# One layer pair on one core: bias rows and inverse blocks passed through DRAM in packed form

## Chip, cores and metric

The kernel runs on one core of one Trainium2 chip. The metric is device time in microseconds, the median of several runs. Times inside an execution are microseconds from the start of its span.

## What is computed

The input is a sequence of 512 tokens of width 1024. A first block (retention, short convolution, three-way sparse attention, gated merge, gated feed-forward with a convolution) and a second block (gated delta rule, sliding-window attention, gated merge, gated feed-forward) are applied in turn. Two pieces of the second block matter here.

The delta rule solves a unit lower triangular system for each chunk of 64 tokens, 4 heads by 8 chunks:

```python
a_mat = jnp.where(strict_lower, jnp.einsum("bhncd,bhnsd->bhncs", k_beta, kc) * decay, 0.0)
lhs = a_mat + jnp.eye(C, dtype=a_mat.dtype)
sol = lax.linalg.triangular_solve(lhs, rhs, left_side=True, lower=True, unit_diagonal=True)
```

The sliding-window branch adds a learned bias that depends only on the distance of query and key, with 8 heads, blocks of 128 queries and 256 keys for each:

```python
dist = SWA_BLOCK + qi - kj
in_window = (dist >= 0) & (dist < WINDOW_2)
bias = rel_bias.astype(jnp.float32)[t5_causal_bucket(dist)]
logits = jnp.where(mask[None, :, None, None], logits + bias, -jnp.inf)
```

## The kernel before, in words

Activations are kept as 128 features by 512 tokens. Each fp32 matrix product runs as three products of rounded high and low parts: `weight` (L274) loads a tile of 128x1024 on SP's queue (L285, two buffers), ScalarE makes the high part `wh` (L268), VectorE the low part `wl` (L269, three buffers each), and `gemm` (L290) issues 24 products of 128x512 (L262) into one of two accumulators `g`. VectorE empties an accumulator in `scaled` (L389). The order on each engine's queue is fixed when the program is built: the framework's scheduler takes the instructions in program order, but moves later ones forward where it reckons them ready. `after` (L234) only tells that scheduler to keep an instruction behind another. An engine takes its queue in order.

**The bias rows.** While the first feed-forward (`ffn1`, L836, 22 turns n, two `gemm` each) runs, `bias_rows(n)` (L1181) is called at the end of each turn. For n = 0 it loads the 32 bucket values of the 8 heads and a one-hot matrix. For n = 1 a product gives 8 rows of 384 bias values, and VectorE copies them to SBUF (L1196). For n = 2 a transfer on GpSimd's queue writes each row 128 times to the DRAM tile `bd` of [8, 128, 384]. For n = 10 to 17 eight transfers write zeros to the DRAM tile `dn_x`. In each turn the gated product is formed on GpSimd (L849), and ScalarE and VectorE split it (L271, L272) into `gh` and `gl`, which only the next stage reads. `bias_table` (L1203) later reads `bd` with a row step of 383, so that partition p has the rows shifted by p: the table `tab` of 128 queries, 8 heads, 256 keys. `swa_head` (L1251) adds it to the scores on VectorE (L1274 for 256 keys, L1276 for the first block's 128).

**The inverse blocks.** `dn_inverse` (L1060) forms 16 strictly lower matrices of 128x128 and writes them to the DRAM tile `dn_n`. `dn_blocks` (L1042) reads the 128 diagonal blocks of 16x16 back, one to a partition (tile N), and inverts them by 15 steps of two VectorE operations (L1053, L1054) into Y. It then writes Y onto the diagonal blocks of the zeroed `dn_x` (L1055) and reads the whole, 16 matrices of 128x128, back as X (L1057), all on SP's queue. `dn_inverse` transposes X on TensorE (L1094) and doubles the inverted blocks to 32, 64 and 128 by products and corrections (L1105, L1109). Between these small products the scheduler sets products of later functions, of `dn_values`, `nat2` and `gates2`, as filler on TensorE.

Of the kernel before, what the change touches and what calls it, by code (L numbers as in the profile page):

```python
# [68 lines left out]
def constants():  # L69
    p = np.arange(128)  # L70
    c = {}
    c["ident"] = np.eye(128)
    c["causal"] = np.concatenate([np.zeros((128, 384)), np.where(p[None] <= p[:, None], 0.0, BIG)], 1)
    t = np.arange(512).reshape(4, 128).T
    cc = np.arange(32)
    c["cmask"] = np.where((16 * cc + 31 <= t[:, :, None]) & (cc < 31), 0.0, -BIG).reshape(128, 128)
    c["any1"] = (p >= 31)[:, None] * np.ones((1, 1))
    theta = 10000.0 ** (-np.linspace(0.0, 1.0, 64, dtype=np.float32))
    ang = np.arange(512, dtype=np.float32)[None, :] * theta.astype(np.float32)[:, None]
    co, si = np.cos(ang.astype(np.float64)), np.sin(ang.astype(np.float64))  # L80
    c["rotc"] = np.concatenate([co, co], 0)
    c["rots"] = np.concatenate([si, -si], 0)
    lg = np.log1p(-(2.0 ** (-5.0 - np.arange(RH))))
    rel = np.arange(512)[None, :] - p[:, None]
    dec = [np.where(rel >= 0, np.exp(lg[h] * np.maximum(rel, 0)), 0.0) * 128 ** -0.5 for h in range(RH)]
    c["decay"] = np.concatenate(dec, 1)
    c["triu"] = (p[:, None] <= p[None, :]) * 1.0
    c["mstrict"] = np.where(p[None, :] < p[:, None], 0.0, -BIG)
    c["mincl"] = np.where(p[None, :] >= p[:, None], 0.0, -BIG)
    lev = []  # L90
    for b in (16, 32, 64):
        cols = (np.arange(64 // b)[:, None] * 2 * b + np.arange(b)[None]).reshape(-1)
        same = (p[:, None] // (2 * b)) == (cols[None] // (2 * b))
        lev.append((same & (p[:, None] % (2 * b) >= b)) * 1.0)
    c["levels"] = np.concatenate(lev, 1)
    c["band"] = (p[:, None] // 32 == np.arange(4)[None]) * 1.0
    return {k: _f(v) for k, v in c.items()}


CONST = constants()  # L100
C_SETS = [["ident"], ["causal", "cmask", "any1", "band"], ["triu", "mstrict", "mincl", "levels"]]
C_OFF, C_LEN = {}, []
for _k, _s in enumerate(C_SETS):
    _o = 0
# [5 lines left out]

def onehot():
    r = np.arange(384)
    dist = 255 - r
    n = np.maximum(dist, 0)
    nf = np.maximum(n, 1).astype(np.float32)
    large = 16 + (np.log(nf / np.float32(16)).astype(np.float32) / np.float32(math.log(8.0)) * np.float32(16)).astype(np.int32)
    large = np.minimum(large, BUCKETS - 1)
    b = np.where(n < 16, n, large)
    m = np.zeros((BUCKETS + 1, 384), np.float32)
    ok = (dist >= 0) & (dist < 128)  # L120
    m[b[ok], r[ok]] = 1.0
    m[BUCKETS, ~ok] = 1.0
    return m
# [72 lines left out]
class Kern:  # L196
# [639 lines left out]
    def ffn1(self):  # L836
        nc, A = self.nc, self.A
        gh, gl = self.units(NF, F32R), self.units(NF, F32R)
        for n in range(NF):
            ta = self.scaled(self.gemm(A["w_fu"][n, 0], self.xh, self.xl))  # L840
            a = self.tmp()
            self.conv(a, ta, V_FC, 3, 44, n)
            th = ta
            nc.scalar.activation(th, a, AF.Tanh, scale=0.5)
            tv = self.scaled(self.gemm(A["w_fu"][n, 1], self.xh, self.xl))
            v = self.tmp()
            self.conv(v, tv, V_FC, 3, 44, NF + n)
            nc.vector.scalar_tensor_tensor(a, th, 1.0, a, op0=OP.add, op1=OP.mult)
            nc.gpsimd.tensor_mul(a, a, v)  # L849
            self.split(gh(n), gl(n), a, 0.5)  # L850
            self.bias_rows(n)
        return gh, gl

    def block1(self):
# [187 lines left out]
    def dn_blocks(self, dn):  # L1042
        nc = self.nc
        zz = lambda: self.sp.tile([128, 16, 16], F32, name="zz", bufs=3)
        N, Y, W = zz(), zz(), zz()
        blocks = lambda d: bass.AP(tensor=d.tensor, offset=d.offset, ap=[[PITCH // 8, 128], [128, 16], [1, 16]])
        nc.sync.dma_start(N, blocks(dn))
        self.after(nc.vector.memset(Y, 0.0), self.last)
        nc.vector.memset(Y.rearrange("p r c -> p (r c)")[:, 0:256:17], 1.0)
        for j in range(15):  # L1050
            a, b = 15 - j, j + 1
            w = W.rearrange("p r c -> p (r c)")[:, :a * b].rearrange("p (r c) -> p r c", c=b)
            nc.vector.tensor_mul(w, N[:, b:, j:b].to_broadcast([128, a, b]), Y[:, j:b, 0:b].to_broadcast([128, a, b]))  # L1053
            self.chain = nc.vector.tensor_sub(Y[:, b:, 0:b], Y[:, b:, 0:b], w)  # L1054
        nc.sync.dma_start(blocks(self.dn_x), Y)  # L1055
        X = self.unit(shape=(128, 16, 128))
        nc.sync.dma_start(X, self.rows_of(self.dn_x))  # L1057
        return X

    def dn_inverse(self):  # L1060
# [117 lines left out]
            nc.vector.tensor_mul(y[:, t], y[:, t], z[:, t])  # L1178
        return y.rearrange("p t h c -> p t (h c)")

    def bias_rows(self, n):  # L1181

        nc, A = self.nc, self.A
        if n == 0:
# [1 line left out]
            rb, oh = self.early[:BUCKETS + 1, 0:8], self.early[:BUCKETS + 1, 128:512]  # L1186
            self.load(rb, A["relb"], self.last)
            self.load(oh, A["oneh"], self.last)
            self.after(nc.gpsimd.memset(self.early[:, 1024:1152], 0.0), self.last)
            self.bias = self.dp.tile([8, 128, 384], F32, name="bd")  # L1190
            self.dn_x = self.dp.tile([16, PITCH], F32, name="dn_x")
        elif n == 1:
            rb, oh = self.early[:BUCKETS + 1, 0:8], self.early[:BUCKETS + 1, 128:512]
            p = self.ps("o", 1)
            self.mm(p[:8, :384], rb, oh, True, True)
            nc.vector.tensor_copy(self.early[:8, 512:896], p[:8, :384])  # L1196
        elif n == 2:
            self.load(self.bias, self.early[:8, None, 512:896].to_broadcast([8, 128, 384]), self.last)
        elif 10 <= n < 18:
            m = slice(2 * (n - 10), 2 * (n - 10) + 2)  # L1200
            self.load(self.rows_of(self.dn_x, m), self.early[:, None, 1024:1152].to_broadcast([128, 2, 128]), self.last)

    def bias_table(self):  # L1203
        self.tab = self.unit(shape=(128, 8, 256))
        dr = self.bias
        src = bass.AP(tensor=dr.tensor, offset=dr.offset + 127, ap=[[383, 128], [128 * 384, 8], [1, 256]])
        self.load(self.tab, src, self.last)

    def swa_proj(self):
# [41 lines left out]
    def swa_head(self, j, s):  # L1251
# [11 lines left out]
        for u in range(2):  # L1263
            lg = self.sp.tile([128, 512], F32, name="sm", bufs=2).rearrange("p (a c) -> p a c", a=2)
            for v in range(2):
# [5 lines left out]
                self.mm(S, st[:, qs], KS[:, 2 + s, k0:k0 + 256], False, True)  # L1271
                i = (j * 4 + nb) * 2 + s
                if nb:
                    nc.vector.scalar_tensor_tensor(lg[:, v, :], S, rr[:, i:i + 1], self.tab[:, h, :], op0=OP.mult, op1=OP.add)  # L1274
                else:
                    nc.vector.scalar_tensor_tensor(lg[:, 0, 128:256], S[:, 0:128], rr[:, i:i + 1], self.tab[:, h, 128:256],  # L1276
                                                   op0=OP.mult, op1=OP.add)
                    nc.gpsimd.tensor_scalar(lg[:, 0, 0:128], lg[:, 0, 128:256], 0.0, -BIG, op0=OP.mult, op1=OP.add)
            us = slice(2 * u, 2 * u + 2)
# [112 lines left out]
```

## Time and profile before

| what | us |
|---|---|
| median of 3 runs | 2077.3 (2075.71 to 2077.73) |
| the profiled execution, own time | 2075.4 |
| its span, first to last instruction | 2073.6 |
| TensorE busy | 2022.6 |
| VectorE busy | 1215.2 |
| ScalarE busy | 846.8 |
| GpSimd busy | 243.7 |

The profile is of one execution. PE is TensorE, PEld its weight loads, DVE is VectorE, ACT ScalarE, POOL GpSimd, SP the engine whose queue issues weight loads. In a row `out<-in` names the tiles, buffer numbers left out: `g`, `s`, `t`, `o` are accumulators, `wf` a loaded weight tile, `u` a large SBUF tile. A bracket at the end of a row gives the idle time of the engine before it and what ended it. "x2" is the number of instructions merged into a row.

### The profile page before, as it was taken

How to read it: one execution, taken by the hardware profiler on the slowest of the kernel's cores; microseconds unless marked ns; L12 is line 12 of the kernel's file. 1: busy time of each engine (PE TensorE's matmuls, PEld its weight loads, DVE VectorE, ACT ScalarE, POOL GpSimd, SP SyncE). 2: the span in 40 equal slices, each digit the busy share in tenths (PEclk: the TensorE clock that was granted, in tenths of full speed). 3: DMA queues.
4: the chain of work that ended last, by engine and by line, in shares of the span. 5: the costliest groups of instructions: out<-in, count | busy, mean ns of one | idle time of the engine just before them, and what ended most of it. 6: DMA issues, size and time to landing. Idle time of an engine off the chain costs nothing.

```text
span 2073.6 us, 26727 instructions
## 1 busy us (share of the span) xinstructions
PE 2022.6 (98%) x10184; PEld 1693.5 (82%) x10184; DVE 1215.2 (59%) x2238; ACT 846.8 (41%) x1530; POOL 243.7 (12%) x369
## 2 busy tenths in 40 slices
PE   7999999999999999998999999999999999999999
PEld 6878888888899888886788888878878878888887
DVE  7477877864525645565777634794557675444422
ACT  4466767742132323332444423553545342222221
POOL 3010011000301111111111100010000121111100
PEclk9999999999999999999999999999999999999999
DMA  6121111123232232344233343322221252322442
GB/s 240 45 72 51 52 52 52 42 83 101 92 108 78 80 99 85 117 157 103 86 108 105 110 136 119 101 77 76 72 82 36 80 184 97 102 93 100 123 126 76
DMA packets 63280, 196.91 MB, mean 95 GB/s; under 512 B 11373, under 2 KB 13549, under 8 KB 62640
## 3 DMA queue, kind: packets, MB, share of 16 engines
q1 hardware_dynamic: 54720, 167.24, 25.2%
q0 software_dynamic: 7712, 26.78, 4.5%
q8 instruction: 80, 1.31, 0.3%
q10 hardware_dynamic: 720, 1.19, 0.2%
q14 instruction: 48, 0.39, 0.1%
HBM read 182.98 MB, written 12.19 MB: 94 GB/s over the span
## 4 chain that ended last, share of the span: by engine, by line
PE 86%; DVE 7%; DMA 3%; ACT 2%; issue 1%; POOL 1%; ACTq 0%; POOLq 0%; DVEq 0%; SPq 0%
PE g L262 72%; PE s L262 5%; PE o L262 5%; DVE wl L269 2%; PE t L656 1%; ACT wh L268 1%; PE t L262 1%; DMA wf<-in_w_fu 1%; DVE w L424 1%; DMA u<-in_xT 1%; DVE u L272 0%; DMA u<-dn_x 0%; PE t L1289 0%; POOL w L591 0%; PE t L698 0%
## 5 line engine op out<-in xcount | busy, mean ns | idle before, releaser
L262 PE MATMUL g<-u,wh 128*128 128x512 f32 x4464 | 1404.9, 393 | 24.7 <-DVE w L389 13.7
L262 PEld LDWEIGHTS g<-u,wh 128*128 128x128 f32 x4464 | 835.6, 189 | 195.3 <-issue 14.4
L262 PE MATMUL g<-u,wl 128*128 128x512 f32 x2232 | 874.7, 392 | 0.2 <-DVE wl L269 0.2
L268 ACT ACTIVATE wh<-wf 128x1024 fp32r<-128x1024 f32 (+4 forms) x325 | 331.7, 1021 | 774.6 <-PE g L262 551.9
L269 DVE TENSOR_TENSOR wl<-wf,wh 128x1024 fp32r<-128x1024 f32 (+4 forms) x325 | 403.7, 1242 | 229.4 <-ACT wh L268 226.2
L262 PEld LDWEIGHTS g<-u,wl 128*128 128x128 f32 x2232 | 420.5, 188 | 85.5 <-DVE wl L269 1.2
L262 PE MATMUL g<-wh,u 128*128 128x256 f32 (+2 forms) x736 | 142.9, 292 | 0.0
L389 DVE TENSOR_TENSOR w<-g,R 128x512 f32<-128x512 f32 x104 | 71.5, 689 | 116.9 <-PE g L262 116.5
L262 PEld LDWEIGHTS g<-wh,u 128*128 128x128 f32 x736 | 117.1, 191 | 1.0 <-DVE u L744 0.2
L424 DVE SCALAR_TENSOR_TENSOR w<-w,vecs 128x510 f32<-128x510 f32 (+1 forms) x140 | 105.6, 754 | 2.9 <-ACT w L422 0.8
L262 PE MATMUL g<-wl,u 128*128 128x256 f32 (+2 forms) x368 | 106.7, 290 | 0.0
L262 PE MATMUL o<-u 128*128 128x256 f32 (+1 forms) x418 | 83.4, 297 | 2.3 <-issue 1.4
L262 PEld LDWEIGHTS o<-u 128*128 128x128 f32 x418 | 61.3, 188 | 14.8 <-ACT u L268 4.6
L262 PE MATMUL s<-u,st 128*128 128x256 f32 (+2 forms) x288 | 71.7, 335 | 0.1
L262 PEld LDWEIGHTS g<-wl,u 128*128 128x128 f32 x368 | 70.2, 191 | 0.8
L268 ACT ACTIVATE u<-t 128x512 fp32r<-128x512 f32 (+1 forms) x112 | 58.2, 528 | 11.0 <-PE t L698 6.3
L1322 POOL TENSOR_TENSOR w<-w,R 128x512 f32<-128x512 f32 x22 | 39.0, 1772 | 198.5 <-ACT w L1321 198.5
L271 ACT ACTIVATE u<-w 128x512 fp32r<-128x512 f32 x44 | 27.3, 623 | 68.2 <-POOL w L849 68.1
L849 POOL TENSOR_TENSOR w<-w 128x512 f32<-128x512 f32 x22 | 28.3, 1284 | 226.2 <-DVE w L424 211.3
L272 DVE SCALAR_TENSOR_TENSOR u<-w,u 128x512 fp32r<-128x512 f32 x44 | 30.2, 689 | 40.9 <-ACT u L271 40.9
L422 ACT ACTIVATE w<-w,vecs 128x512 f32<-128x512 f32 x64 | 46.2, 721 | 19.6 <-DVE w L389 15.0
L262 PEld LDWEIGHTS s<-u,st 128*128 128x128 f32 x288 | 47.0, 189 | 5.3 <-DVE sm L1276 0.5
(376 smaller groups left out, 1914.3 us busy)
## 6 DMA issues: line engine op xcount, KB each, us to landing
wf<-in_w_fu SPq DMA_DIRECT2D x44, 512.0 KB, 3.5
wf<-in_x_gu SPq DMA_DIRECT2D x44, 512.0 KB, 3.7
wf<-in_w_sc SPq DMA_DIRECT2D x24, 512.0 KB, 3.6
wf<-in_w_mg SPq DMA_DIRECT2D x24, 512.0 KB, 3.6
wf<-in_w_fd SPq DMA_DIRECT2D x16, 512.0 KB, 3.6
wf<-in_x_gt SPq DMA_DIRECT2D x16, 512.0 KB, 3.7
wf<-in_x_dn SPq DMA_DIRECT2D x16, 512.0 KB, 3.6
x<-st POOLq DMA_DIRECT2D x24, 256.0 KB, 2.4
```

The costliest lines, as they stand in the source:

```text
L262: self.last = self.nc.tensor.matmul(out, l, r, start=start, stop=stop)
L268: nc.scalar.activation(hi, src, AF.Copy)
L269: nc.vector.tensor_sub(lo, src, hi.bitcast(F32))
L271: nc.scalar.activation(hi, src, AF.Copy, scale=scale)
L272: return nc.vector.scalar_tensor_tensor(lo, src, scale, hi.bitcast(F32), op0=OP.mult, op1=OP.subtract)
L389: self.nc.vector.tensor_mul(t, p, self.R)
L422: nc.scalar.activation(dst, src, AF.Copy, scale=self.vec(w + (nt - 1) * stride + j))
L424: nc.vector.scalar_tensor_tensor(dst[:, i:], src[:, :T - i], self.vec(w + (nt - 1 - i) * stride + j), dst[:, i:], op0=OP.mult, op1=OP.add)
L656: nc.tensor.transpose(pt[:, c:c + 128], parts[v][:, k * 128:(k + 1) * 128], self.ident)
L849: nc.gpsimd.tensor_mul(a, a, v)
L1322: nc.gpsimd.tensor_mul(t, t, self.R)
```

## The change

The one-hot matrix is built for distances that rise along the row (r - 128 in place of 255 - r), and the 8 rows of 384 are written once to DRAM, in the call for n = 1. The table is read with a row step of one element, so that neighbouring partitions read overlapping pieces of the same rows, and `swa_head` reads the table backwards along the keys (step -1). The inverted blocks are written to DRAM as they lie (128 blocks of 256 numbers) and read back with 16 numbers for each row and matrix (tile XB, 128x16x16). Four multiplications on VectorE, one for each group of four matrices, spread XB over the 128 columns of X with a mask of 128x8 block indicators, which joins the constants. The zeroed `dn_x`, its zero fills and their memset go.

```diff
--- before.py
+++ after.py
@@ -94,11 +94,12 @@
         lev.append((same & (p[:, None] % (2 * b) >= b)) * 1.0)
     c["levels"] = np.concatenate(lev, 1)
     c["band"] = (p[:, None] // 32 == np.arange(4)[None]) * 1.0
+    c["diag"] = (p[:, None] // 16 == np.arange(8)[None]) * 1.0
     return {k: _f(v) for k, v in c.items()}
 
 
 CONST = constants()
-C_SETS = [["ident"], ["causal", "cmask", "any1", "band"], ["triu", "mstrict", "mincl", "levels"]]
+C_SETS = [["ident"], ["causal", "cmask", "any1", "band"], ["triu", "mstrict", "mincl", "levels", "diag"]]
 C_OFF, C_LEN = {}, []
 for _k, _s in enumerate(C_SETS):
     _o = 0
@@ -110,7 +111,7 @@
 
 def onehot():
     r = np.arange(384)
-    dist = 255 - r
+    dist = r - 128
     n = np.maximum(dist, 0)
     nf = np.maximum(n, 1).astype(np.float32)
     large = 16 + (np.log(nf / np.float32(16)).astype(np.float32) / np.float32(math.log(8.0)) * np.float32(16)).astype(np.int32)
@@ -848,7 +849,7 @@
             nc.vector.scalar_tensor_tensor(a, th, 1.0, a, op0=OP.add, op1=OP.mult)
             nc.gpsimd.tensor_mul(a, a, v)
             self.split(gh(n), gl(n), a, 0.5)
-            self.bias_rows(n)
+            self.bias_row(n)
         return gh, gl
 
     def block1(self):
@@ -1052,9 +1053,16 @@
             w = W.rearrange("p r c -> p (r c)")[:, :a * b].rearrange("p (r c) -> p r c", c=b)
             nc.vector.tensor_mul(w, N[:, b:, j:b].to_broadcast([128, a, b]), Y[:, j:b, 0:b].to_broadcast([128, a, b]))
             self.chain = nc.vector.tensor_sub(Y[:, b:, 0:b], Y[:, b:, 0:b], w)
-        nc.sync.dma_start(blocks(self.dn_x), Y)
+        dx = self.dp.tile([128, 16, 16], F32, name="dn_x")
+        nc.sync.dma_start(dx, Y)
         X = self.unit(shape=(128, 16, 128))
-        nc.sync.dma_start(X, self.rows_of(self.dn_x))
+        XB = self.sp.tile([128, 16, 16], F32, name="zz", bufs=3)
+        nc.sync.dma_start(XB, bass.AP(tensor=dx.tensor, offset=dx.offset, ap=[[16, 128], [2048, 16], [1, 16]]))
+        diag = self.const("diag")[:, None, :, None].to_broadcast([128, 4, 8, 16])
+        for h in range(4):
+            ms = slice(4 * h, 4 * h + 4)
+            nc.vector.tensor_mul(X[:, ms, :].rearrange("p m (b c) -> p m b c", c=16),
+                                 XB[:, ms, None, :].to_broadcast([128, 4, 8, 16]), diag)
         return X
 
     def dn_inverse(self):
@@ -1178,7 +1186,7 @@
             nc.vector.tensor_mul(y[:, t], y[:, t], z[:, t])
         return y.rearrange("p t h c -> p t (h c)")
 
-    def bias_rows(self, n):
+    def bias_row(self, n):
 
         nc, A = self.nc, self.A
         if n == 0:
@@ -1186,24 +1194,18 @@
             rb, oh = self.early[:BUCKETS + 1, 0:8], self.early[:BUCKETS + 1, 128:512]
             self.load(rb, A["relb"], self.last)
             self.load(oh, A["oneh"], self.last)
-            self.after(nc.gpsimd.memset(self.early[:, 1024:1152], 0.0), self.last)
-            self.bias = self.dp.tile([8, 128, 384], F32, name="bd")
-            self.dn_x = self.dp.tile([16, PITCH], F32, name="dn_x")
+            self.bias = self.dp.tile([8, 384], F32, name="bd")
         elif n == 1:
             rb, oh = self.early[:BUCKETS + 1, 0:8], self.early[:BUCKETS + 1, 128:512]
             p = self.ps("o", 1)
             self.mm(p[:8, :384], rb, oh, True, True)
             nc.vector.tensor_copy(self.early[:8, 512:896], p[:8, :384])
-        elif n == 2:
-            self.load(self.bias, self.early[:8, None, 512:896].to_broadcast([8, 128, 384]), self.last)
-        elif 10 <= n < 18:
-            m = slice(2 * (n - 10), 2 * (n - 10) + 2)
-            self.load(self.rows_of(self.dn_x, m), self.early[:, None, 1024:1152].to_broadcast([128, 2, 128]), self.last)
+            self.load(self.bias, self.early[:8, 512:896], self.last)
 
     def bias_table(self):
         self.tab = self.unit(shape=(128, 8, 256))
         dr = self.bias
-        src = bass.AP(tensor=dr.tensor, offset=dr.offset + 127, ap=[[383, 128], [128 * 384, 8], [1, 256]])
+        src = bass.AP(tensor=dr.tensor, offset=dr.offset + 1, ap=[[1, 128], [384, 8], [1, 256]])
         self.load(self.tab, src, self.last)
 
     def swa_proj(self):
@@ -1271,9 +1273,9 @@
                 self.mm(S, st[:, qs], KS[:, 2 + s, k0:k0 + 256], False, True)
                 i = (j * 4 + nb) * 2 + s
                 if nb:
-                    nc.vector.scalar_tensor_tensor(lg[:, v, :], S, rr[:, i:i + 1], self.tab[:, h, :], op0=OP.mult, op1=OP.add)
+                    nc.vector.scalar_tensor_tensor(lg[:, v, :], S, rr[:, i:i + 1], self.tab[:, h, ::-1], op0=OP.mult, op1=OP.add)
                 else:
-                    nc.vector.scalar_tensor_tensor(lg[:, 0, 128:256], S[:, 0:128], rr[:, i:i + 1], self.tab[:, h, 128:256],
+                    nc.vector.scalar_tensor_tensor(lg[:, 0, 128:256], S[:, 0:128], rr[:, i:i + 1], self.tab[:, h, 127::-1],
                                                    op0=OP.mult, op1=OP.add)
                     nc.gpsimd.tensor_scalar(lg[:, 0, 0:128], lg[:, 0, 128:256], 0.0, -BIG, op0=OP.mult, op1=OP.add)
             us = slice(2 * u, 2 * u + 2)
```

## Rows read from the trace of the kernel before

**Rows 1.** The page, busy time of TensorE: us, share of the span, instructions.

```profile
PE 2022.6 (98%) x10184; PEld 1693.5 (82%) x10184; DVE 1215.2 (59%) x2238; ACT 846.8 (41%) x1530; POOL 243.7 (12%) x369
```

**Rows 2.** The chain that ended last, in order of time: start, length, what.

```profile
946.70 22.01 DMA wf<-in_w_fu
...
1411.25 2.97 DMA dn_x<-zz
1414.35 6.49 DMA u<-dn_x
```

**Rows 3.** Busy time by stretch: stretch, engines with instructions started, clock, DMA share, GB/s.

```profile
960.00:970.00 10.00, 5.83 (x26) 4.51 (x24) 0.11 (x1) 1.20 (x2) 0.00 (x0) 0.94 0.49 80
970.00:980.00 10.00, 5.25 (x15) 4.19 (x15) 6.90 (x9) 3.57 (x5) 0.38 (x1) 0.55 0.58 128
980.00:990.00 10.00, 7.87 (x35) 6.20 (x33) 4.41 (x5) 3.65 (x6) 0.91 (x1) 1.00 0.38 138
990.00:1000.00 10.00, 7.40 (x25) 6.01 (x26) 9.58 (x14) 3.91 (x7) 1.29 (x1) 0.83 0.18 52
...
1040.00:1050.00 10.00, 10.00 (x46) 8.28 (x45) 6.89 (x10) 4.27 (x6) 2.02 (x2) 1.00 0.35 113
```

**Rows 4.** Timeline of TensorE around the two pauses: start, length, what, idle before.

```profile
974.75 1.19 PE L262 MATMUL g<-u,wh 128*128 128x512 f32 x2 [8.93 <-DVE w L389]
...
979.53 0.62 PE L262 MATMUL g<-u,wh 128*128 128x512 f32 x2
...
987.02 0.61 PE L262 MATMUL g<-u,wh 128*128 128x512 f32 x2
...
992.60 1.19 PE L262 MATMUL g<-u,wh 128*128 128x512 f32 x2 [4.74 <-DVE w L389]
...
996.34 0.63 PE L262 MATMUL g<-u,wh 128*128 128x512 f32 x2
```

**Rows 5.** DMA issues: all loads of w_fu, then 940 to 982 us; median to landing.

```profile
wf<-in_w_fu SPq DMA_DIRECT2D x44, 512.0 KB, 3.5
...
wf<-in_w_fu SPq DMA_DIRECT2D x5, 512.0 KB, 8.0
bd<-u POOLq DMA_DIRECT2D x1, 1536.0 KB, 34.4
```

**Rows 6.** Timelines of GpSimd and ScalarE between the pauses.

```profile
953.27 1.28 POOL L849 TENSOR_TENSOR w<-w 128x512 f32<-128x512 f32 x1 [8.65 <-DVE w L424]
...
968.80 1.06 ACT L268 ACTIVATE wh<-wf 128x1024 fp32r<-128x1024 f32 x1 [17.80 <-DMA wf<-in_w_fu]
...
988.64 1.13 ACT L271 ACTIVATE u<-w 128x512 fp32r<-128x512 f32 x2
```

**Rows 7.** Timelines of TensorE and VectorE where X comes back.

```profile
1420.88 1.09 PE L1094 MATMUL t<-c,u 128*128 128x128 f32 x8 [3.44 <-DMA u<-dn_x]
...
1423.80 0.42 DVE L1105 TENSOR_TENSOR zz<-s,c 128x256 f32<-128x256 f32 x1 [7.26 <-PE s L262]
```

**Rows 8.** DMA issues of the whole span: count, KB each, median us to landing.

```profile
dn_n<-u SPq DMA_DIRECT2D x4, 256.0 KB, 2.3
...
u<-in_rows POOLq DMA_DIRECT2D x1, 512.0 KB, 5.7
...
zz<-dn_n SPq DMA_DIRECT2D x1, 128.0 KB, 3.6
```

**Rows 9.** The page, groups of instructions: busy us and mean ns of one.

```profile
L272 DVE SCALAR_TENSOR_TENSOR u<-w,u 128x512 fp32r<-128x512 f32 x44 | 30.2, 689 | 40.9 <-ACT u L271 40.9
```

**Rows 10.** The table: its load, its first use, and VectorE operations at wide and unit step.

```profile
L242 POOL DMA_DIRECT2D u<-bd x1: 955/955/955, 1455.4 to 1455.4; - x1
...
L1276 DVE SCALAR_TENSOR_TENSOR sm<-s,swr,u x8: 342/348/352, 1548.3 to 1601.1; 128x128 f32<-128x128 f32 x8
...
L442 DVE TENSOR_SCALAR u<-u,vecs 128x124 f32<-128x124 f32 x31 | 8.1, 328 | 0.0
...
L456 DVE TENSOR_SCALAR zz<-w 128x128 f32<-128x128 f32 x2 | 0.4, 223 | 0.0
```

## The prediction

> **What bounds the kernel now.** I read the page first. TensorE is busy for 98% of the span [rows 1], so an edit pays only where TensorE stands still or runs slowly, and what is saved on another engine is worth nothing by itself. The second view is the chain that ended last, in order of time, searched for links that are not TensorE. Two of them belong to transfers that this change touches. From 946.70 us it runs for 22.01 us over a weight load of the first feed-forward stage. From 1411.25 us it runs over the write of the inverse blocks (2.97 us) and from 1414.35 us over their read back (6.49 us) [rows 2]. The other views were then asked about these two places only.
>
> The first place, by stage: in an ordinary stretch of this stage TensorE starts 46 products in 10 us. In the four stretches from 960 to 1000 us it starts 26, 15, 35 and 25, and in two of them the granted clock is 0.55 and 0.83 [rows 3]. The timeline of TensorE shows why: it stood idle for 8.93 us before 974.75 and for 4.74 us before 992.60 [rows 4]. After each pause it ran at the lower of its two levels: between 979.53 and 987.02 us there are 11 groups of three products, 0.68 us each, but the four groups from 974.75 to 979.53 take 4.78 us and the three from 992.60 to 996.34 take 3.74 us.
>
> What it waited for: the bias write (bd, 1.5 MB, issued on GpSimd's queue) takes 34.4 us to land, and the weight loads beside it take 8.0 us in the median, against 3.5 us for all loads of this stage [rows 5]. ScalarE's split of such a weight tile came at 968.80 us, after 17.80 us of waiting for the load [rows 6]. VectorE takes its work in order, so the low-half split and the evacuation behind it (L389), which frees the accumulator for TensorE, were late too. The second pause is a consequence: GpSimd had the gated product (L849) done soon after 953.27, but ScalarE took the split that reads it (L271) only at 988.64 us, behind five weight splits [rows 6].
>
> The second place: the transposes of X begin at 1420.88 us, after 3.44 us in which TensorE idled for the read [rows 7]; its filler products had run out at 1417.4.
>
> **Part 1, the bias write.** Eight rows go out once instead of 128 times, 12 KB instead of 1.5 MB; in proportion to the measured write that is 34.4 / 128 = 0.27 us of transfer, far too little to hold up a 512 KB load. Gone are the two pauses, 8.93 + 4.74 = 13.67 us, and the slow groups, 4.78 - 4 x 0.68 = 2.06 and 3.74 - 3 x 0.68 = 1.70 us. Together 17.4 us. The check by counts: 4 x 46 - 101 = 83 products missing, 83 / 4.6 = 18.0 us. What is late next is nothing: the same loop runs from 1040 us on with TensorE at 10.00 of 10 us, with the zero-fill transfers beside it [rows 3]. From below I keep 11.0 us: the first pause and its slow groups alone (8.93 + 2.06), if the order of ScalarE's queue still delays the second. From above 18.0 us. The write is now issued in the call for n = 1 and waits on GpSimd for the copy of its eight rows. Behind it on that queue stands at most the next L849, and behind that L271 on ScalarE; one copy is shorter than the 0.69 us of [rows 9], and the product itself is read only in the next stage, so I cost this at nothing.
>
> **Part 2, the inverse blocks.** Removed: the write scattered into a zeroed matrix and the 1 MB read. Added: one contiguous 128 KB write, a 128 KB read in 64-byte runs, and four multiplications of 128x512 on VectorE. The write: 2.97 us scattered at most; four stores of 256 KB from the same queue take 2.3 us in the median [rows 8]. I take 2.3, being nearest in queue and form. The read has the very shape of the read of N at the head of this function (128 partitions, 16 runs of 64 bytes), which lands in 3.6 us [rows 8]. Issue after landing costs 1414.35 - 1411.25 - 2.97 = 0.13 us. One multiplication is 0.69 us by the 128x512 two-operand form on VectorE [rows 9], and I allow 0.2 us for two handovers. The first four matrices are ready at 1411.25 + 2.3 + 0.13 + 3.6 + 0.2 + 0.69 = 1418.17, against 1420.88: 2.7 us sooner. The other three multiplications end 0.7 us apart, where the transposes came in pairs of heads 1.3 us apart; that may expose 0.2 us. I take 2.5 us of the 3.44. Bounds: at best all 3.44 us. At worst there is a loss of 3 us: the filler products that now run between the read's issue at 1414.35 [rows 2] and 1417.4 us hang on weight splits on VectorE, and if those are queued behind multiplications that wait for the read, the pause starts at 1414.4 instead. In the trace of before VectorE stands idle for 7.26 us up to 1423.80 [rows 7], so the four multiplications (2.8 us) displace nothing there. On SP's queue the weight loads behind the read leave sooner, not later.
>
> The Trainium skill (DMA: Bandwidth & Descriptors, Specifications) gives 512 bytes as the least transfer for full rate, which speaks against 64-byte runs in place of 512-byte ones. Taken to mean that the short runs win nothing over the long ones, it gives a read of 6.49 us, the first matrices at 1421.06 and a loss of 0.2 us for Part 2. The row of N's read speaks against that here: 3.6 us, with an eighth of the bytes.
>
> **Part 3, what is hidden.** The eight zero fills and a memset on GpSimd vanish under a TensorE that is full there [rows 3]. Eight more columns of constants ride in a load that has 576 already: nothing. The overlapping read of the bias table is 1 MB out of 12 KB. The nearest row is the load of one 4 KB row to all 128 partitions, 512 KB in 5.7 us [rows 8], so an estimate of 11.4 us for twice as much. It is issued at 1455.4 and first read at 1548.3 us [rows 10]: 93 us of cover. Price taken: 0.
>
> **Part 4, the mirrored read.** 24 additions of 256 and 8 of 128 elements take the table backwards, 7168 elements. No row shows a negative step. Bounds: nothing (the step is one element); or the price of a wide step, an operation of 124 elements at step 16 taking 328 ns against 223 ns for 128 dense ones [rows 10], 0.85 ns per element, 6.1 us, if all of it falls on the path. A gain has no reason. I take 0, the nearer in distance stepped.
>
> **Sum.** 17.4 + 2.5 = 19.9 us. The profiled execution took 2075.4 us (span 2073.6), so it would become 2055.5. It lies 1.9 us below the median of the runs, 2077.3; from that median the forecast is 2077.3 - 19.9 = 2057.4 us.
>
> **The rivals.** (a) The second pause stays, because the order of the engines' queues, which the framework's scheduler fixes at build time, keeps five weight splits ahead of L271: 2077.3 - 11.0 - 2.5 = 2063.8. For it: that order is in the trace. Against: it stands in no other turn of the loop, so it looks like the scheduler's answer to the large write. (b) The mirrored read costs its upper bound: 2057.4 + 6.1 = 2063.5. VectorE is not free in that stage, but most of the steps hide behind TensorE. (c) The weight loads were late for another reason than the bias write, and only Part 2 pays: 2077.3 - 2.5 = 2074.8, no change that can be told. Against it: the slow loads lie inside the 34.4 us of the write and nowhere else in the loop. (d) Slower: all 1024 pieces of the overlapping read hit the same 12 KB, and the read is as disruptive per us as the bias write was, 17.4 / 34.4 = 0.5 us of TensorE lost per us. It eats the gain at 40 us and makes the kernel measurably slower from 48 us on; at 55 us the time is 2057.4 + 28 = 2085. The row of 5.7 us is for a still narrower source and speaks against it by a factor of four. (e) The packed read is no faster than the wide one, 6.49 us: 1411.25 + 2.3 + 0.13 + 6.49 + 0.89 = 1421.06, 0.2 us late, and 2077.3 - 17.4 + 0.2 = 2060.1 us. N's read of the same shape speaks against it.
>
> **How the numbers follow.** Forecast 0.68, (a) 0.10, (b) 0.08, (c) 0.05, (d) 0.03, (e) 0.06. What can be told from no change is 0.2%, 4.2 us: faster is below 2073.1, slower above 2081.5. Faster: forecast, (a), (b) and (e), 0.92; same 0.05; slower 0.03. The range: below, 18.0 + 3.4 instead of 19.9, and some 4 us for the scheduler's other choices in the rest of the kernel, where pauses of 1 to 2 us are common in the chain: 2052. Above, (a) with the loss of 3 us in Part 2 falls at 2069; I go to 2066, which takes in (a) and (b) by themselves.
>
> **What would show it.** Right: no link over a weight load near 947 us in the chain, TensorE at 10.00 in each stretch from 960 to 1000 us at full clock, weight loads near 3.5 us; a read of the packed blocks landing in about 3.6 us, four multiplications near 0.69 us, a pause of under 1 us before the transposes; the additions with the table at the same length as now (0.348 us for 128 elements [rows 10]). Wrong: a new pause in that loop, TensorE waiting for VectorE at the multiplications, or a table read of tens of us with late weights beside it.

## The result, and the profile of the changed kernel

The changed kernel takes 2055.36 us in the median of 5 runs (2054.83 to 2056.85). The kernel before, run beside it, takes 2077.73 (5 runs, 2075.71 to 2081.04). The ratio is 0.989, with a 95% interval of 0.9879 to 0.99: 22.4 us, where 19.9 were forecast. The profiled execution took 2054.83 us, its span 2053.1. Line numbers of the changed kernel are one higher up to the inverse (L263 is the L262 of before, L272 the L271, L390 the L389), eight higher behind it (L1102 is the L1094) and two higher where the table is used (L1278 is the L1276). L1064 holds the new multiplications.

Busy time by stretch, as in [rows 3], of the changed kernel:

```profile
960.00:970.00 10.00, 10.00 (x46) 8.29 (x45) 7.34 (x10) 4.32 (x6) 1.29 (x1) 1.00 0.27 87
970.00:980.00 10.00, 10.00 (x46) 8.29 (x45) 6.92 (x10) 4.67 (x6) 1.29 (x1) 1.00 0.33 103
980.00:990.00 10.00, 10.00 (x46) 8.29 (x45) 6.89 (x10) 4.25 (x6) 1.29 (x1) 1.00 0.33 105
990.00:1000.00 10.00, 10.00 (x46) 8.29 (x45) 6.89 (x10) 4.27 (x6) 1.29 (x1) 1.00 0.32 107
```

TensorE starts 46 products in each stretch, at the full granted clock, where it started 26, 15, 35 and 25. The DMA issues from 940 to 982 us, as in [rows 5], show why:

```profile
wf<-in_w_fu SPq DMA_DIRECT2D x8, 512.0 KB, 3.5
bd<-u POOLq DMA_DIRECT2D x1, 12.0 KB, 1.7
```

The bias write lands in 1.7 us, not in 34.4, and the eight weight loads beside it in 3.5 us like all others of this stage. The chain that ended last has lost its weight load near 947 us, and the two links of [rows 2] at the inverse are shorter (start, length, what):

```profile
938.82 340.49 PE g L263 x1508
...
1393.20 1.69 DMA dn_x<-zz
1394.91 2.77 DMA zz<-dn_x
1398.46 1.26 PE t L1102 x8
```

From 938.82 us the chain runs over 1508 products of TensorE without a break. The write of the inverse blocks takes 1.69 us (2.97 before), the read 2.77 (6.49 before). Timelines of VectorE and TensorE at that place, as in [rows 7]:

```profile
1397.71 2.50 DVE L1064 TENSOR_TENSOR u<-zz,c 128x512 f32<-128x512 f32 x4 [0.97 <-DMA zz<-dn_x]
...
1398.46 1.26 PE L1102 MATMUL t<-c,u 128*128 128x128 f32 x8 [0.91 <-DVE u L1064]
...
1400.53 1.22 DVE L270 TENSOR_TENSOR wl<-wf,wh 128x1024 fp32r<-128x1024 f32 x1
```

TensorE waits 0.91 us for the first of the four multiplications, in place of 3.44 us for the read. The last row is a weight split that stands behind the four multiplications on VectorE; it comes back in the working below.

Where the 20.5 us between the two profiled spans (2073.6 and 2053.1) lie: the write of the inverse blocks is issued at 1411.25 us before and at 1393.20 after, so 18.05 us were won ahead of it. Of these, 17.36 are there at the end of the first feed-forward (the first weight load of the stage behind it, w_fd, is issued at 1154.42 and 1137.06 us), and 0.68 come in the stage that loads x_qkv, whose twelve loads are issued over 63.54 us before and 62.86 after; the change edits nothing in that stage. The other 2.45 us are won between the write and the end of the delta rule, and nothing behind it. So 19.8 of the 20.5 us lie where the two parts of the change are.

### The profile page after: what moved, and what is told of

The parts are those of the page before. It is cut to its first block, busy times and chain, and to the rows that moved or that the text cites. A ratio compares the mean times of both kernels' runs of the same rounds, so it can differ in the third digit from the quotient of the medians.

```text
span 2053.1 us, 26719 instructions
## 1 busy us (share of the span) xinstructions
PE 2018.5 (98%) x10184; PEld 1691.2 (82%) x10184; DVE 1215.9 (59%) x2242; ACT 847.4 (41%) x1530; POOL 238.5 (12%) x360
## 4 chain that ended last, share of the span: by engine, by line
PE 89%; DVE 6%; ACT 2%; DMA 1%; issue 1%; POOL 0%; ACTq 0%; DVEq 0%; POOLq 0%
PE g L263 74%; PE s L263 5%; PE o L263 5%; DVE wl L270 2%; PE t L657 1%; ACT wh L269 1%; PE t L263 1%; DMA u<-in_xT 1%; DVE u L273 0%; DVE w L425 0%; PE t L1291 0%; POOL w L592 0%; PE t L699 0%; DVE u L270 0%; PE t L595 0%
## 5 line engine op out<-in xcount | busy, mean ns | idle before, releaser
L263 PE MATMUL g<-u,wh 128*128 128x512 f32 x4464 | 1402.5, 392 | 11.5 <-ACT u L272 9.7
L263 PEld LDWEIGHTS g<-u,wh 128*128 128x128 f32 x4464 | 834.2, 188 | 181.1 <-ACT u L272 10.6
L263 PE MATMUL g<-u,wl 128*128 128x512 f32 x2232 | 873.5, 391 | 0.2 <-DVE wl L270 0.2
L269 ACT ACTIVATE wh<-wf 128x1024 fp32r<-128x1024 f32 (+4 forms) x325 | 331.7, 1020 | 746.2 <-PE g L263 547.4
L263 PEld LDWEIGHTS g<-u,wl 128*128 128x128 f32 x2232 | 419.7, 188 | 85.1 <-DVE wl L270 1.2
L263 PE MATMUL g<-wh,u 128*128 128x256 f32 (+2 forms) x736 | 142.9, 292 | 0.0
L390 DVE TENSOR_TENSOR w<-g,R 128x512 f32<-128x512 f32 x104 | 71.5, 688 | 115.5 <-PE g L263 115.4
L263 PEld LDWEIGHTS g<-wh,u 128*128 128x128 f32 x736 | 117.1, 191 | 1.0 <-DVE u L745 0.2
L263 PE MATMUL g<-wl,u 128*128 128x256 f32 (+2 forms) x368 | 106.8, 290 | 0.0
L263 PE MATMUL o<-u 128*128 128x256 f32 (+1 forms) x418 | 83.3, 297 | 2.3 <-issue 1.4
L263 PEld LDWEIGHTS o<-u 128*128 128x128 f32 x418 | 61.4, 189 | 14.7 <-ACT u L269 4.6
L263 PE MATMUL s<-u,st 128*128 128x256 f32 (+2 forms) x288 | 71.7, 335 | 0.1
L263 PEld LDWEIGHTS g<-wl,u 128*128 128x128 f32 x368 | 70.2, 191 | 0.8
L269 ACT ACTIVATE u<-t 128x512 fp32r<-128x512 f32 (+1 forms) x112 | 58.2, 528 | 11.1 <-PE t L699 6.3
L272 ACT ACTIVATE u<-w 128x512 fp32r<-128x512 f32 x44 | 27.4, 623 | 77.4 <-POOL w L850 77.3
L850 POOL TENSOR_TENSOR w<-w 128x512 f32<-128x512 f32 x22 | 28.3, 1288 | 208.4 <-DVE w L425 208.4
L263 PEld LDWEIGHTS s<-u,st 128*128 128x128 f32 x288 | 47.0, 189 | 5.3 <-DVE sm L1278 0.5
```

The source lines that it names most:

```text
L263: self.last = self.nc.tensor.matmul(out, l, r, start=start, stop=stop)
L269: nc.scalar.activation(hi, src, AF.Copy)
L272: nc.scalar.activation(hi, src, AF.Copy, scale=scale)
L390: self.nc.vector.tensor_mul(t, p, self.R)
```

## The experiments

The experiments are e1 to e10. e1 to e4 had runs of the kernel before beside them with a median of 2077.83 us (17 runs, 2074.59 to 2081.2), e5 to e8 with 2080.41 us (8 runs, 2078.09 to 2081.39); each is compared with its own.

| kernel | median (from, to), us | ratio, 95% interval | gain, us |
|---|---|---|---|
| e1, bias part alone | 2058.86 (2057.45, 2060.14) | 0.9906 [0.9892, 0.9919] | 19.0 |
| e2, inverse part alone | 2073.91 (2072.74, 2075.55) | 0.9977 [0.9968, 0.9986] | 3.9 |
| e3, 64 copies | 2072.6 (2071.09, 2073.29) | 0.9974 [0.9962, 0.9985] | 5.2 |
| e4, 32 copies | 2060.94 (2059.04, 2061.61) | 0.9915 [0.9901, 0.9928] | 16.9 |
| e5, 1.5 MB from 128 partitions | 2060.49 (2058.8, 2061.49) | 0.9904 [0.989, 0.9919] | 19.9 |
| e6, split order held | 2074.3 (2071.84, 2075.87) | 0.9969 [0.9956, 0.9982] | 6.1 |
| e7, changed kernel with zero fills | 2056.24 (2055.12, 2057.06) | 0.9883 [0.9867, 0.99] | 24.2 |
| e8, 1.5 MB in 16 pieces | 2060.55 (2058.9, 2062.06) | 0.9905 [0.9891, 0.992] | 19.9 |

### The two parts by themselves

e1 is the kernel before with the bias part of the change alone:

```diff
-            self.bias = self.dp.tile([8, 128, 384], F32, name="bd")
+            self.bias = self.dp.tile([8, 384], F32, name="bd")
...
-        elif n == 2:
-            self.load(self.bias, self.early[:8, None, 512:896].to_broadcast([8, 128, 384]), self.last)
+            self.load(self.bias, self.early[:8, 512:896], self.last)
...
-        src = bass.AP(tensor=dr.tensor, offset=dr.offset + 127, ap=[[383, 128], [128 * 384, 8], [1, 256]])
+        src = bass.AP(tensor=dr.tensor, offset=dr.offset + 1, ap=[[1, 128], [384, 8], [1, 256]])
```

> The kernel before with the bias part of the change alone (12 KB written once, overlapping and mirrored read); zero fills, scattered write and 1 MB read of the inverse blocks stay. Theory (the pauses in the feed-forward came from the bias write): spans shrink by 18.0 us, the distance from the write of the inverse blocks to the transposes stays at 9.6 us with 3.4 us of pause, time about 2059.5 where the kernel before takes 2077.5. Rival (part of the gain belongs to the zero fills or the freed buffer of the inverse part): less than 17 us. Rival (the inverse part needs the bias part or the other way round): the two parts alone do not add up to the 20.5 us by which the span of the whole change is shorter.

The distances of the one-hot matrix and the mirrored read go with it. e2 is the changed kernel with all of these lines turned back, so that the inverse part remains.

> The changed kernel with the bias part undone: 1.5 MB written 128 times, forward read; packed inverse blocks and no zero fills. Theory: the pauses of 8.9 and 4.7 us in the feed-forward are back, the pause before the transposes is 0.9 us in place of 3.4, time 2.5 us under the kernel before, 2075.0. Rival (the zero fills cost something beside full TensorE): 4 us or more under the kernel before. Rival (the packed path gains only by a scheduling accident that the bias part brought): within 1 us of the kernel before.

In e1 TensorE is at 10.00 of 10 us with 46 products from 960 to 1000 us, and its span is 2055.8, 17.8 us under that of before; the inverse is as it was (read 6.29 us, pause 3.23). In e2 both pauses are back. Timeline of TensorE in e2:

```profile
975.93 1.19 PE L263 MATMUL g<-u,wh 128*128 128x512 f32 x2 [8.84 <-DVE w L390]
...
993.78 1.17 PE L263 MATMUL g<-u,wh 128*128 128x512 f32 x2 [4.74 <-DVE w L390]
...
1417.55 1.26 PE L1102 MATMUL t<-c,u 128*128 128x128 f32 x8 [0.84 <-DVE u L1064]
```

What follows: each part does its work alone, and they add up, 19.0 + 3.9 = 22.9 us against 22.4 together, as closely as intervals of some 17 to 22 us for e1 and 2.9 to 6.6 for e2 can tell. The inverse part gives 1.4 us more by medians than the 2.5 us of the forecast, near the 4 us of e2's rival, that the zero fills cost something. e7 speaks against that rival, and e9 shows another source of such a difference.

### How long the bias write is

e3 and e4 write each bias row 64 and 32 times instead of 128 and read the table in two and four pieces:

```diff
-            self.bias = self.dp.tile([8, 128, 384], F32, name="bd")
+            self.bias = self.dp.tile([8, 64, 384], F32, name="bd")
...
-        src = bass.AP(tensor=dr.tensor, offset=dr.offset + 127, ap=[[383, 128], [128 * 384, 8], [1, 256]])
-        self.load(self.tab, src, self.last)
+        for p0 in range(0, 128, 64):
+            src = bass.AP(tensor=dr.tensor, offset=dr.offset + 127 - p0, ap=[[383, 64], [64 * 384, 8], [1, 256]])
+            self.load(self.tab[p0:p0 + 64], src, self.last)
```

> The kernel before with 64 copies of each bias row in place of 128 (0.75 MB), the table read in two loads that reuse the copies; the result is unchanged. Theory A (loss in proportion to the write, 0.5 us of TensorE per us of write): write lands in 17 us, loss 8.7 to 9 us, time about 2068.5. Theory B (the prefetched weight tiles cover a fixed time and only what exceeds it is lost; the write lands 35 us after issue and TensorE lost 17.7, so the cover is some 17 us): write lands in 17 us, loss 0 to 2 us, time 2060 to 2062.

> The same with 32 copies (0.375 MB) and four table loads. Theory A (in proportion): write lands in 8.6 us, loss 4.4 us, time about 2064. Theory B (fixed cover): loss 0, time as with the bias part of the change alone, 2059.5.

The write of e3 lands in 17.8 us, that of e4 in 9.8 us. Timeline of TensorE in e3:

```profile
968.71 0.70 PE L262 MATMUL g<-u,wh 128*128 128x512 f32 x2 [2.67 <-DVE w L389]
...
986.20 1.19 PE L262 MATMUL g<-u,wh 128*128 128x512 f32 x2 [4.74 <-DVE w L389]
```

The first pause shrank from 8.93 to 2.67 us, but the second is 4.74 us, as long as before to a hundredth. So half the write keeps most of the loss (a gain of 5.2 us of 19), which neither theory of e3 had: the loss is not in proportion to the write, and it is not one pause. In e4 there is no pause in the loop, 10.00 of 10 us in each stretch, and nearly the whole gain. Once there is a second pause, its length does not follow the length of the write; e6 looks for its cause.

### Bytes, or the partitions they come from

e5 writes the same 1.5 MB from 128 partitions instead of 8. It leaves out the bias values of the heads: the partitions from 8 on hold zeros, which the memset now writes there.

```diff
-            self.after(nc.gpsimd.memset(self.early[:, 1024:1152], 0.0), self.last)
+            self.after(nc.gpsimd.memset(self.early[:, 512:1152], 0.0), self.last)
...
-            self.load(self.bias, self.early[:8, None, 512:896].to_broadcast([8, 128, 384]), self.last)
+            self.load(self.bias.rearrange("h p c -> p h c"), self.early[:, None, 512:896].to_broadcast([128, 8, 384]), self.last)
```

> The kernel before with the same 1.5 MB bias write, but issued from 128 SBUF partitions of 12 KB each (8 rows of 384) instead of from 8 partitions of 192 KB each. The bias values of the heads are left out (the partitions from 8 on hold zeros), so the table is not the reference's; the bytes, the count of rows in DRAM and everything behind the table are as before. Two runs of the last series bear on it: 64 copies (0.75 MB, 17.8 us to land) kept most of the loss, 32 copies (0.375 MB, 9.8 us) had none. Theory A, the write is slow and disturbs because it leaves from 8 partitions only: by the 512 KB weight loads, 3.5 us from 128 partitions, 1.5 MB should land in some 3 x 3.5 = 10.5 us, which is near the 9.8 us that did no harm: no pause of TensorE between 960 and 1000 us, 2060 us (the kernel before less the 17.8 us that the bias part gave by spans), at most 2 us more. Theory B, the bytes themselves hold up the weight loads whatever partitions they come from: the write lands in over 25 us, weight loads beside it take 8 us in the median again, TensorE pauses for some 9 us, and the time stays near 2077.

DMA issues of e5 from 930 to 1160 us, and one stretch of its table by windows:

```profile
wf<-in_w_fu SPq DMA_DIRECT2D x37, 512.0 KB, 3.5
...
bd<-u POOLq DMA_DIRECT2D x1, 1536.0 KB, 7.1
```

```profile
960.00:970.00 10.00, 10.00 (x46) 8.29 (x45) 7.49 (x10) 3.98 (x5) 1.29 (x1) 1.00 0.26 79
```

The write lands in 7.1 us, and there is no pause. Theory A holds: 1.5 MB from 128 partitions are no trouble, from 8 they are. By the two rows the write goes at 1.57 MB / 34.4 us = 46 GB/s from 8 partitions and at 1.57 MB / 7.1 us = 222 GB/s from 128, 4.8 times as fast. The queue that carried the write shows two reasons (940 to 982 us; packets, MB, share of 16 engines), first before, then in e5:

```profile
q0 software_dynamic: 704, 1.58, 34.9%
```

```profile
q0 software_dynamic: 368, 1.57, 11.7%
```

34.9% of 16 engines over 42 us are 235 us of engine time, 6.8 engines over the write's 34.4 us; in e5 it is 79 us, 11.1 engines over 7.1 us. A rule of the Trainium skill (DMA: Bandwidth & Descriptors, Rules for kernel authors) bears on that part: a transfer whose outermost dimension has fewer than 16 entries is confined to at most that many DMA engines. The 6.8 agree with at most 8. The larger part is that one engine moved 1.58 MB / 235 us = 6.7 GB/s from 8 partitions and 20 GB/s from 128; why is not shown.

### One write, or sixteen small ones

e8 keeps the 8 partitions and the bytes, but sends 8 copies in each of 16 turns:

```diff
-        elif n == 2:
-            self.load(self.bias, self.early[:8, None, 512:896].to_broadcast([8, 128, 384]), self.last)
+        if 2 <= n < 18:
+            self.load(self.bias[:, 8 * n - 16:8 * n - 8], self.early[:8, None, 512:896].to_broadcast([8, 8, 384]), self.last)
```

> The kernel before with the same 1.5 MB, from the same 8 partitions, but in 16 transfers of 8 copies (96 KB), one in each of the turns 2 to 17 of the first feed-forward, instead of one transfer in turn 2. A turn is some 13 us, and by the one write's 34.4 us a sixteenth lands in 2.2 us. Theory A, what costs is a write that holds up several weight loads in a row (32 copies, 9.8 us, cost nothing): no pause in the loop, 2060, at most 2 us more. Theory B, each us of such a write costs TensorE about half a us wherever it stands: 16 x 2.2 x 0.52 = 18 us, so 2077 as before.

DMA issues of e8 from 930 to 1160 us:

```profile
wf<-in_w_fu SPq DMA_DIRECT2D x37, 512.0 KB, 3.5
...
bd<-u POOLq DMA_DIRECT2D x16, 96.0 KB, 3.6
```

Sixteen writes of 3.6 us are 58 us of write, more than the one of 34.4, and TensorE is at 10.00 of 10 us in each stretch from 940 to 1020 us. So it is not the sum of the write's time that costs. What fits all the runs is that one slow transfer costs when it outlasts the cover of the two weight buffers; by e4 and e3 that cover ends somewhere between a write of 9.8 us and one of 17.8 us.

### What makes the second pause

e6 keeps the 1.5 MB write of the kernel before and only holds back the weight split of the second half of turn n until the gated product of turn n-2 has been split (`G` collects the latter instructions):

```diff
-            nc.scalar.activation(hi, src, AF.Copy)
+            self.after(nc.scalar.activation(hi, src, AF.Copy), self.hold)
...
-            tv = self.scaled(self.gemm(A["w_fu"][n, 1], self.xh, self.xl))
+            tv = self.scaled(self.gemm(A["w_fu"][n, 1], self.xh, self.xl, hold=self.G[n - 2] if n > 1 else None))
```

> The kernel before, the 1.5 MB write as it is, with one ordering rule more: the weight split on ScalarE of the second half of turn n stays behind the split of the gated product of turn n-2. In the kernel before, five weight splits stand ahead of two gated products after the bias write; here the two gated products come ahead of the late weight splits. TensorE's order in this stretch is the same. Theory A, the second pause (4.74 us, and 1.70 us of slow products behind it) is made by that order alone: it goes, the first pause (8.9 us, then slow products) stays, and the time is 2077.8 - 6.4 = 2071.4. Theory B, the second pause is the late weight loads' own: a pause of 4 us or more stays behind the first one, and the time is within 2 us of the kernel before.

Timelines of ScalarE and TensorE in e6:

```profile
962.33 0.62 ACT L271 ACTIVATE u<-w 128x512 fp32r<-128x512 f32 x1
965.49 0.63 ACT L271 ACTIVATE u<-w 128x512 fp32r<-128x512 f32 x1 [2.54 <-POOL w L849]
...
969.25 1.06 ACT L268 ACTIVATE wh<-wf 128x1024 fp32r<-128x1024 f32 x1 [1.45 <-DMA wf<-in_w_fu]
...
970.36 0.88 PE L262 MATMUL g<-u,wh 128*128 128x512 f32 x2 [4.04 <-ACT wh L268]
...
977.24 1.22 PE L262 MATMUL g<-u,wh 128*128 128x512 f32 x2 [6.00 <-ACT wh L268]
```

The two gated products are split (L271) before the late weight tiles, at 962 and 965 us instead of 988.64. The weight loads are as late as before and TensorE waits 4.04 + 6.00 us for them, where it waited 8.93. By its letter the 6.00 is theory B's pause behind the first one. But both end with the split of a late weight tile, where the second pause of before, at 992.60 us, ended with the evacuation (L389). No pause follows there: from 980 to 1000 us TensorE is at 10.00 of 10 us, and the kernel is 6.1 us faster, where theory A has 6.4 and theory B at most 2. So with the write in place another order on ScalarE's queue is enough to remove the pause at 992.60 us; the waits for the loads themselves come to 10.04 us, 1.1 more than the first pause of before.

### The zero fills

e7 is the changed kernel with the eight fills and their memset put back, to a tile that nobody reads:

```diff
+        elif 10 <= n < 18:
+            m = slice(2 * (n - 10), 2 * (n - 10) + 2)
+            self.load(self.rows_of(self.zf, m), self.early[:, None, 1024:1152].to_broadcast([128, 2, 128]), self.last)
```

> The changed kernel with the eight zero fills (128 KB each) and their memset put back on GpSimd in the turns 10 to 17 of the first feed-forward, to a DRAM tile that nobody reads. The prediction gave them no cost, since TensorE was full in that stretch: 2055.4, within 2 us, TensorE at 10.00 of 10 us in every stretch from 1000 to 1060 us. Rival: the fills collide with weight loads as the bias write did; a fill lands in 2.3 us, and by the bias write's 17.8 us lost per 34.4 us that would be 8 x 2.3 x 0.52 = 9.5 us, so 2065.

The fills land in 2.2 us each, TensorE is at 10.00 of 10 us in each stretch from 1000 to 1060 us, and the median is 2056.24 against 2055.36: no difference that these runs can tell. Their removal was worth nothing that shows.

### Two more profiles of the kernel before

e9 and e10 are the kernel before without any edit.

> The kernel before, unchanged, for a second profile of it. Its runs spread from 2074.6 to 2081.4 us, and over the runs the time goes with the mean granted clock of the execution (0.998 at 2074.6, 0.993 at 2081.4); the changed kernel's runs spread over 2 us only, at 0.999 to 1.0. The first profile was of a quick one (2075.4). Theory A, what varies is how long TensorE stays at its lower level behind the two pauses: a run of 2078 or more shows the same pauses (8.9 and 4.7 us), but more slow products between 974 and 1010 us, and windows outside that stretch hold the full clock. Theory B, the lower clock turns up in other stages, unconnected with the bias write: the stretch from 960 to 1010 us has the counts of the first profile, and windows at other places show a clock below 1.00.

> The same again, a third profile of the kernel before, with the same two theories: A, the extra time of the longer runs lies in slow products behind the pauses at 974 and 992 us; B, it lies at other places.

e9 took 2078.71 us, e10 2074.56. Both have the same two pauses (8.89 and 4.74; 8.88 and 4.74 us), and e9 has the counts of [rows 3] from 970 to 1000 us to within one product. What differs lies elsewhere. Windows of e9, then of the first profile of the kernel before:

```profile
970.00:980.00 10.00, 5.16 (x15) 4.10 (x16) 6.91 (x9) 3.58 (x5) 0.30 (x1) 0.56 0.62 127
...
1420.00:1430.00 10.00, 10.00 (x60) 9.59 (x60) 2.40 (x4) 3.94 (x6) 0.00 (x0) 0.70 0.36 129
```

```profile
1420.00:1430.00 10.00, 9.12 (x74) 8.54 (x74) 3.25 (x6) 3.60 (x6) 0.00 (x0) 1.00 0.42 152
```

Behind the pause at the inverse, e9's clock is 0.70 of full and TensorE starts 60 products where the other execution starts 74. The timeline of TensorE in e9:

```profile
1419.86 1.97 PE L1094 MATMUL t<-c,u 128*128 128x128 f32 x8 [3.09 <-DMA u<-dn_x]
...
1428.58 0.60 PE L1112 MATMUL t<-c,u 128*128 128x128 f32 x4
```

The same eight transposes take 1.97 us, against 1.09 us in [rows 7]. From their start to the first L1112 it is 8.72 us here and 5.98 us there (1420.88 to 1426.86), with the same 46 products between: the lower level cost 2.74 us. For e9 theory B holds, and A falls. In the nine profiles with the wide read back (before, e1, e3, e4, e5, e6, e8, e9, e10) these transposes come after a pause of 3.1 to 3.5 us; in six of them they run slowly (1.67 to 1.97 us), in three not (1.09 us). In the three profiles with the packed read (after, e2, e7) the pause is 0.84 to 0.95 us, and the eight take 1.26 us with the clock at 1.00 in all three. A second such place, near 1670 us in the kernel before, is not touched by the change: two pauses of 1.07 and 0.52 us, with a clock of 0.83 behind them in e9 and 1.00 in the first profile and in e10. The two profiles' offset is 1.75 us at 1669 us and 3.3 us at the end, so it cost e9 some 1.55 us. The clock is below 1.00 behind it in seven of the twelve profiles, e2 and e7 with the packed read among them. The two places together do not account for the whole spread of the kernel before: of its 17 runs beside e1 to e4 four took 2074.59 to 2074.94 us and the others 2077.01 to 2081.2, the longest some 2.5 us more than e9, and no profile is of so long a run.

## Why the prediction came out as it did

**Part 1, 17.4 us, measured 17.36 at the end of the feed-forward.** e1's span is 17.8 us under that of before. The loop itself, from its first gated product on GpSimd to its last, took 246.1 us before (931.2 to 1177.3) and takes 228.4 (931.6 to 1160.0), 17.7 less; it began 0.4 us later. Both ways of counting, pauses and slow groups (17.4) and missing products (18.0), were good to 0.4 us. The mechanism is shown: without the slow write both pauses go, and with it they come back (e2). Nothing came late in their place: the write is issued at 940.25 us on GpSimd, and L850 behind it starts at 942.68, where L849 started at 942.26 before, a shift that the loop's later start has already. The price of the write was put at 0.27 us by proportion and measured 1.7 us, still far under the 9.8 us that e4 shows to be harmless. Proportion left out a fixed part: the four writes from 8 partitions (96 to 1536 KB in 3.6 to 34.4 us) lie near a line of some 1.5 us and 0.0214 us per KB, an estimate that gives 1.8 us for 12 KB. The account was also incomplete: it spoke of 1.5 MB, but e5 shows that the same bytes from 128 partitions are harmless.

**Part 2, 2.5 us, measured 2.45 in the two profiled executions, 3.9 by the medians of e2.** The size there is right, by terms that were not. The write took 1.69 us (2.3 in the sum), the read 2.77 (3.6), the four multiplications 2.50 us together (0.69 each, some 2.8). The row of N's read that stood for the packed read takes 3.6 us in the changed kernel too; it is issued 0.5 us behind a weight load, which may be why it is longer, but no run parts the two. The first matrices were thus ready 1398.46 - 1393.20 = 5.26 us after the write's issue, against 1420.88 - 1411.25 = 9.63: 4.4 us sooner, not 2.7. But TensorE idled only 2.53 us less, since part of the filler that used to stand in front of the transposes now comes behind them: twelve products of the next weights ran there before, some 0.23 us each, and four run there now, because the second weight split on VectorE is the row at 1400.53 us, behind the four multiplications. That is the queueing that the lower bound of -3 us was made from; it cost 1.8 of the 4.4 us. The prediction had TensorE waiting for VectorE at the multiplications as a sign of being wrong, and a pause of under 1 us as a sign of being right; both came. That 2.5 met 2.45 is in part luck: steps up to the first matrices that were 1.7 us quicker than in the sum, against 1.8 us of filler that it did not charge.

What the prediction left out is a term that it never wrote down: it took the price of this pause as its idle time. In e9 the clock falls behind the pause, and then it cost 2.74 us more. With that in six of nine profiles it would be 1.8 us on average, an estimate from these few, five of which are of edited kernels; of the three of the kernel before itself one shows it. That is of the size of what is missing, 2.0 us between the forecast of 2057.4 and the 2055.36 measured and 1.4 between 2.5 and the 3.9 of e2, but an average is set against medians here, and the account fits without being proven. The four runs of e1, which keeps the wide read, fit it too: two took 2057.45 and 2057.6 us, the second of them profiled with the clock up at both places, and two took 2060.11 and 2060.14, some 2.6 more. The trace that I had was of an execution in which the clock stayed up (2075.4 us, 1.9 below the median); I noted the 1.9 us and subtracted the same gain from both, where the median may hold a cost that the profile did not. For Part 1 the lower level behind the pauses was counted, because that profile showed it.

**Part 3, nothing, measured nothing.** e7 for the fills. The overlapping read, by the DMA issues of the changed kernel:

```profile
u<-bd POOLq DMA_DIRECT2D x1, 1024.0 KB, 7.3
```

It is as quick from 12 KB of overlapping rows as it was from 1.5 MB of separate ones (7.5 us), and well below the estimate of 11.4.

**Part 4, nothing, measured nothing.** Groups of VectorE in the changed kernel, then in the kernel before (busy us, mean ns):

```profile
L1276 DVE SCALAR_TENSOR_TENSOR sm<-s,swr,u 128x256 f32<-128x256 f32 x24 | 11.0, 473 | 0.2 <-PE s L263 0.2
L1278 DVE SCALAR_TENSOR_TENSOR sm<-s,swr,u 128x128 f32<-128x128 f32 x8 | 2.8, 347 | 1.6 <-PE t L1291 1.6
```

```profile
L1274 DVE SCALAR_TENSOR_TENSOR sm<-s,swr,u 128x256 f32<-128x256 f32 x24 | 11.0, 473 | 0.2 <-PE s L262 0.2
L1276 DVE SCALAR_TENSOR_TENSOR sm<-s,swr,u 128x128 f32<-128x128 f32 x8 | 2.8, 347 | 1.6 <-PE t L1289 1.6
```

Reading the table backwards takes the same mean time, to a nanosecond.

**The rivals.** (a), the second pause stays by the queue's order: its mechanism is real (e3, e6), but the order belonged to the large write, as the argument against it said, and went with it: in the changed kernel ScalarE splits the gated product at 965.89, 976.77 and 987.65 us, once in each turn. (b) falls by the two groups above. (c) falls by e1, e5 and e8: without that one write, or with its bytes sent in another form, the weight loads land in 3.4 to 3.5 us. (d) falls by the 7.3 us. (e), the packed read no faster: 2.77 us against 6.49. It rested on the rule of the Trainium skill (DMA: Bandwidth & Descriptors, Specifications) that transfers under 512 bytes lose rate; with an eighth of the bytes in 64-byte runs the read was still 2.3 times as quick, though per byte it was slower (0.13 MB / 2.77 us = 47 GB/s against 1.05 MB / 6.49 us = 162 GB/s). So the fewer bytes outweighed whatever the short runs cost. How it would stand at equal bytes no run shows.

**What stays open.** What decides in one execution whether the clock falls behind a pause of 3 us was not found. The length of the pause does not part the two cases: 3.09 us brought it down in e9, 3.44 us left it up in the first profile. The remaining 0.91 us at the inverse was left as it is, being less than these runs can tell apart.

## What to carry to other kernels

Look at a transfer's shape as well as its bytes: the one that left from 8 partitions was slow here, and where it lasted longer than the buffers of the stream beside it, it stopped the engine that the stream feeds, and the scheduler's order around it added a pause of its own. Cutting it up and spreading it over the partitions both removed the harm. Before a gain read from one trace is taken off a median, compare that execution's time and clock with the median's: if it was a quick one, a pause in it may cost more in the others than its idle time.

## What the runs showed of the chip

A wait of 3.1 to 3.5 us on TensorE brought its granted clock down behind it in six of nine profiles and left it up in three, with the same products behind (a wait of 3.09 us brought it down in e9, one of 3.44 us left it up in the first profile); at the lower level, 1.2 GHz, the eight transposes took 1.97 us instead of 1.09. The Trainium skill (TensorE: Matmul & The Clock Gate, HAM oscillation) warns that waits for data let TensorE fall back to half rate for the work behind them; the six agree, and the three add that a wait of much the same length does so in some executions only. And a DMA of 96 KB from 8 partitions takes 3.6 us, one of 384 KB 9.8 us, of 768 KB 17.8 us and of 1536 KB 34.4 us, while 1536 KB from 128 partitions takes 7.1 us.
